# Head norms and memory softmax worked in place in PSUM, with small copies and scalings on ScalarE, in a two-layer hybrid decoder trunk

## The chip, the cores and the metric

The kernel runs on one core of one Trainium2 chip. It is timed as device microseconds of one execution, and the figure given is the median of several runs. Five engines matter: PE (TensorE: matmuls and transposes), DVE (VectorE), ACT (ScalarE), POOL (GpSimd) and SP, which issues the DMAs. SBUF is the working memory; PSUM holds the matmuls' results, in eight banks of 512 fp32 values for each of 128 partitions. Each engine runs its own instructions in a fixed order and waits on semaphores for the others.

## The reference

Two layers over 512 tokens of width 1024, all in fp32. Only what bears on the change is shown: rms norms of the heads with partial rotary embedding, the attention into 256 memory tokens, and the compressed branch of the sparse attention.

```python
def memory_attention(q, mem_n, w_kv, qnorm, knorm):
    k, v = jnp.split(mem_n @ w_kv, 2, axis=-1)
    q = rms_norm(q.reshape(Bz, S, M_HEADS, HEAD_DIM), qnorm)
    k = rms_norm(k.reshape(Bz, -1, M_HEADS, HEAD_DIM), knorm)
    s = jnp.einsum('bshd,bmhd->bhsm', q, k) * (HEAD_DIM ** -0.5)
    p = jax.nn.softmax(s, axis=-1)
    return jnp.einsum('bhsm,bmhd->bshd', p, v).reshape(Bz, S, M_WIDTH)
...
def even_layer(x, mem_n, pos, ...):
    q = rms_norm(b_q.reshape(Bz, S, B_HEADS, 2, B_QK_DIM), b_qnorm).transpose(0, 2, 3, 1, 4)
    k = rms_norm(b_k.reshape(Bz, S, B_HEADS, 2, B_QK_DIM), b_knorm).transpose(0, 2, 3, 1, 4)
    q, k = rope_partial(q, pos), rope_partial(k, pos)
...
def nsa(q, kv, gates, pos, ...):
    q = rope_partial(rms_norm(q, qnorm).transpose(0, 2, 1, 3), pos).reshape(Bz, G, R, S, hd)
    vc = compress(v_cmp_raw, cmp_idx, cmp_pos_v, cmp_w1_v, cmp_w2_v).transpose(0, 2, 1, 3)
...
def odd_layer(x, mem_n, pos, ...):
    gates = jax.nn.sigmoid(d_bg.reshape(Bz, S, D_HEADS, 3))
```

Layer 0 joins a chunked gating unit, a differential attention (8 heads of 32) and the memory attention (4 heads of 64). Layer 1 joins a convolution with 31 taps, a sparse attention (8 query heads of 64, compressed, selected and window branches) and again the memory attention. Each layer ends in one output projection.

## The kernel before

Tokens are taken in four tiles of 128. Every weight is fetched as fp32 and split into a high and a low half of the fast fp32r type: ACT copies the high half (L376), and the low half is the difference (L377), on POOL for the weights (tiles of 128x1024) and on DVE for activations. A product is then three matmuls (L396, L397, L398). PE does almost nothing else: transposes are matmuls too (L393).

The program is written as generators for the pieces of a layer (`mem_kv`, `b_qk`, `m_attn`, `d_kv`, `d_q`, `d_cmp`, `out_part` ...), which `merge` interleaves by rates and lead constants. The order in which each engine runs its instructions is then set at build by a list scheduler with priorities; nothing is reordered while it runs. A PSUM bank comes from a small pool of pages ("d", "t", "s", "c") and is given back once its last reader is done.

The pieces that the change touches:

- `head_norm` (L488): for 4 or 8 heads of 64. A projection's bank `p` is squared on ACT (L492), summed on DVE (L494), POOL makes the reciprocal root (`rstd`, L370 and L372), DVE multiplies `p` by gains or cosines into the SBUF tile `t` (L498 without rotary, L501 with), by sines into `u` (L503), and adds `u` crosswise to `t` (L504, L505). From there on the bank is free. It is called for the memory keys (`mem_kv`), the memory queries (`m_query`, used by `m_q` in layer 0 and `m_q1` in layer 1), the keys (`d_kv`) and queries (`d_q`) of layer 1: 12 passes without and 8 with rotary.
- `to_keys` (L511) and `to_queries` (L521) multiply `t` by the reciprocal root in SBUF; PE transposes the result, and L529/L530 copy it out as high and low halves (L530 on DVE).
- `b_qk` (L871 to L887) does the same for layer 0's heads of 32, in 16 passes: L873, L875, L878, L880, L881, L882, and at last L883, SBUF to SBUF.
- `m_attn` (L588): for each of two pairs of heads of a token tile, scores (L597/L598) into the bank `s`, the maximum (L600, DVE), exp (L603, ACT) into the SBUF tile `e`, the reciprocal of the sums (L604, DVE), and the scaling of `e` in place by `times`: the first head on DVE (L572), the second on POOL (L570). PE transposes `e`, and L582 to L584 multiply with the values. There are 16 such passes.
- `d_cmp` (L1111, L1115): compressed values copied to SBUF on ACT, and from there eight times 32x64 by DVE. `m_q1` (L1134): the gates' last step, DVE.

The convolution works around all this: for two of its four channel tiles, DVE adds 30 taps in PSUM (L1260); for one, ACT scales a tap (L1257) into one of two tiles `tmp`, and POOL adds it (L1258), so ACT's tap waits for POOL's add of two taps earlier.

## Time and profile before

| | |
|---|---|
| three runs, median (lowest to highest) | 735.17 us (733.96 to 738.78) |
| the profiled execution | 736.76 us, of which the span is 734.7 us |
| PE busy | 673.6 us, 92% of the span |
| DVE busy | 534.5 us, 73% |
| POOL busy | 388.5 us, 53% |
| ACT busy | 366.9 us, 50% |
| mean granted clock of TensorE | 0.979 of full speed |

Busy shares are averages over the whole span. A PE that counts as busy also counts the part of a matmul that overlaps the next one, so the idle time before single PE rows, given in brackets behind them with the instruction that ended it, tells more than the sum.

### The profile page before, as it was taken

What the parts mean: (1) busy time and instruction counts of PE and PEld (TensorE: products, weight loads), DVE (VectorE), ACT (ScalarE), POOL (GpSimd) and SP (SyncE); (2) the same over time, 40 slices, a digit from 0 to 9 for tenths busy, and PEclk for the clock granted to TensorE, in tenths of its full rate; (3) what the DMA queues carried; (4) which work ended last, traced back from release to release, by engine and by line L of the source; (5) the groups of instructions that cost most, each with busy time, mean ns of one, the idle gap of its engine ahead of it and who ended that gap; (6) DMA issues with size and microseconds to landing.
All of it is one profiled execution on the core that took longest, in us unless ns stands there. A gap on an engine that the chain in (4) does not pass through costs nothing.

```text
span 734.7 us, 10935 instructions
## 1 busy us (share of the span) xinstructions
PE 673.6 (92%) x3819; PEld 571.1 (78%) x3819; DVE 534.5 (73%) x1216; ACT 366.9 (50%) x819; POOL 388.5 (53%) x343
## 2 busy tenths in 40 slices
PE   4999999999999888999899899698697989989997
PEld 3789998788899767888787777586586878777885
DVE  4607787767867788952749939997959678888773
ACT  5344354555464664732534466432425566665651
POOL 3376985554366469524647389963625233511450
PEclk9999999999999999999999999999898999999999
DMA  8542254643231435222223111022211011110121
GB/s 307 162 143 73 69 148 111 186 115 119 72 116 59 143 115 200 76 71 58 92 86 118 56 58 58 29 90 83 83 34 58 29 58 31 63 52 1 58 72 72
DMA packets 22375, 66.55 MB, mean 91 GB/s; under 512 B 3504, under 2 KB 3760, under 8 KB 22320
## 3 DMA queue, kind: packets, MB, share of 16 engines
q1 hardware_dynamic: 22320, 65.86, 27.4%
q8 instruction: 30, 0.49, 0.3%
q14 instruction: 25, 0.20, 0.1%
HBM read 57.46 MB, written 2.10 MB: 81 GB/s over the span
## 4 chain that ended last, share of the span: by engine, by line
PE 59%; DVE 23%; POOL 7%; issue 4%; ACT 4%; DMA 2%; SPq 0%; POOLq 0%; DVEq 0%; ACTq 0%
PE banks L396 15%; PE banks L397 15%; PE banks L398 15%; PE banks L393 5%; DVE banks L1260 4%; PE banks L923 3%; DVE arena_r L377 2%; POOL arena_f L372 2%; POOL arena_r L377 2%; DMA arena_f<-in_wall_dram 2%; PE banks L1211 2%; ACT arena_r L376 2%; DVE arena_f L925 2%; PE banks L961 1%; POOL arena_f L1258 1%
## 5 line engine op out<-in xcount | busy, mean ns | idle before, releaser
L396 PE MATMUL banks<-arena_r 128*128 128x512 f32 (+2 forms) x784 | 293.5, 380 | 13.9 <-DVE arena_f L473 3.3
L397 PE MATMUL banks<-arena_r 128*128 128x512 f32 (+2 forms) x784 | 292.2, 374 | 4.2 <-POOL arena_r L377 3.1
L398 PE MATMUL banks<-arena_r 128*128 128x512 f32 (+2 forms) x784 | 290.7, 373 | 0.6 <-POOL arena_r L377 0.5
L377 POOL TENSOR_TENSOR arena_r<-arena_f,arena_r 128x1024 fp32r<-128x1024 f32 (+2 forms) x87 | 211.2, 2436 | 143.9 <-ACT arena_r L376 141.3
L396 PEld LDWEIGHTS banks<-arena_r 128*128 128x128 f32 x784 | 150.6, 193 | 40.3 <-ACT arena_r L376 5.2
L397 PEld LDWEIGHTS banks<-arena_r 128*128 128x128 f32 x784 | 150.4, 192 | 28.0 <-POOL arena_r L377 4.0
L398 PEld LDWEIGHTS banks<-arena_r 128*128 128x128 f32 x784 | 150.1, 192 | 24.7 <-POOL arena_r L377 1.4
L376 ACT ACTIVATE arena_r<-arena_f 128x1024 fp32r<-128x1024 f32 (+2 forms) x131 | 110.4, 854 | 80.8 <-PE banks L398 19.3
L393 PE MATMUL banks<-const,arena_f 128*128 128x128 f32 x507 | 83.5, 281 | 28.0 <-DVE arena_f L411 9.6
L393 PEld LDWEIGHTS banks<-const,arena_f 128*128 128x128 f32 x507 | 62.6, 146 | 39.0 <-DVE arena_f L411 10.1
L377 DVE TENSOR_TENSOR arena_r<-banks,arena_r 128x512 fp32r<-128x512 f32 (+1 forms) x112 | 67.0, 608 | 26.1 <-ACT arena_r L376 25.6
L376 ACT ACTIVATE arena_r<-banks 128x512 fp32r<-128x512 f32 (+1 forms) x112 | 57.8, 532 | 43.9 <-PE banks L393 27.1
L925 DVE CUSTOM_DVE_ANT_0 arena_f<-banks,const 128x512 f32<-128x512 f32 (+3 forms) x128 | 60.2, 484 | 21.1 <-PE banks L923 15.1
L372 POOL TENSOR_TENSOR arena_f<-arena_f,const 128x4 f32<-128x4 f32 (+3 forms) x60 | 68.6, 1146 | 3.6
L570 POOL TENSOR_SCALAR arena_f<-arena_f 128x256 f32<-128x256 f32 (+3 forms) x48 | 29.0, 609 | 74.2 <-DVE arena_f L1190 25.2
L1260 DVE SCALAR_TENSOR_TENSOR banks<-arena_f,const,banks 128x482 f32<-128x482 f32 (+14 forms) x90 | 66.0, 733 | 1.4
L954 ACT ACTIVATE arena_f<-arena_f 128x512 f32<-128x512 f32 (+3 forms) x64 | 35.8, 560 | 45.8 <-DVE arena_f L925 45.4
L923 PE MATMUL banks<-arena_r 128*128 128x512 f32 (+7 forms) x192 | 51.5, 345 | 4.2 <-DVE arena_f L925 4.1
L653 DVE TENSOR_TENSOR arena_f<-arena_f,banks 128x512 f32<-128x512 f32 x40 | 27.3, 684 | 29.0 <-PE banks L398 28.3
L1188 ACT ACTIVATE arena_f<-arena_f 128x512 f32<-128x512 f32 (+3 forms) x64 | 35.6, 558 | 24.2 <-DVE arena_f L925 24.2
L370 POOL TENSOR_SCALAR arena_f<-arena_f 128x4 f32<-128x4 f32 (+3 forms) x60 | 19.0, 317 | 47.9 <-DVE arena_f L494 15.8
L923 PEld LDWEIGHTS banks<-arena_r 128*128 128x128 f32 (+1 forms) x192 | 33.1, 193 | 9.0 <-DVE arena_f L925 5.9
(175 smaller groups left out, 847.0 us busy)
## 6 DMA issues: line engine op xcount, KB each, us to landing
arena_f<-in_wall_dram SPq DMA_DIRECT2D x88, 512.0 KB, 3.3
arena_r<-arena_r SPq DMA_DIRECT2D x96, 64.0 KB, 2.0
arena_f<-in_x_dram SPq DMA_DIRECT2D x7, 512.0 KB, 4.6
arena_f<-in_w_dram SPq DMA_DIRECT2D x4, 512.0 KB, 3.9
out_dram<-arena_f SPq DMA_DIRECT2D x8, 256.0 KB, 2.0
arena_f<-in_norms_dram SPq DMA_DIRECT2D x3, 512.0 KB, 4.7
arena_f<-in_mem_dram SPq DMA_DIRECT2D x2, 512.0 KB, 3.2
arena_f<-in_wqb_dram SPq DMA_DIRECT2D x2, 420.0 KB, 3.3
```

The lines of the kernel that those rows point to most:

```text
L372: G.tensor_tensor(r, v, mhalf[:parts, :n], ALU.pow)
L376: act(h, src, AF.Copy)
L377: (eng or V).tensor_tensor(l, src, f32(h), SUB)
L393: nc.tensor.transpose(o, i, ident[:k, :k])
L396: mm(o, lh, rh, start=first, stop=False)
L397: mm(o, lh, rl, start=False, stop=False)
L398: mm(o, ll, rh, start=False, stop=last)
L923: mm(t[:, a % per, :], q, k[:, :w], start=b == 0, stop=b == len(qk) - 1)
L925: V.tensor_tensor_reduce(e[a], t[:, a % per, :], cmask[:, S - w:], -1.0, -NEG, ADD, ALU.min, nm[:, a:a + 1])
L954: act(e[m], e[m], AF.Exp, bias=nm[:, m:m + 1], scale=-1.0, accum_out=l[:, i, m:m + 1])
L1188: act(es[j], es[j], AF.Exp, bias=nm[:, j:j + 1], scale=-1.0, accum_out=l[:, j:j + 1])
L1260: V.scalar_tensor_tensor(acc[:, z:], hc[:, :S - z], cw[:, f, k:k + 1], acc[:, z:], MUL, ADD)
```

## The change

All of `head_norm`'s and `b_qk`'s products and rotary adds are now written back into the projection's bank, and the last multiplication (`to_keys`, `to_queries`, L883) reads the bank and writes SBUF. The sine product is moved ahead of the in-place cosine product. In `m_attn` the exp is written in place into the score bank; the scaling reads the bank and writes `e`, on DVE for the first head and on ACT (a Copy with a per-partition scale) for the second; POOL has no part in it any more. The eight copies of `d_cmp` go from PSUM to their place on ACT, with the factor 0.5 in them, and so does the last step of the gates. The product with lambda in the differential attention (L957, L958) is as it was. Of the diff, what is left out are the callers, which only hand the three results of `head_norm` on.

```diff
@@ head_norm
         act(sq, p3, AF.Square)
+        if rope is not None:
+            cg, sg = rope
+            u = sc([P, nh, 16])
+            V.tensor_tensor(u, p3[:, :, 0:16], bc(sg.unsqueeze(1), [P, nh, 16]), MUL)
         ss = sc([P, nh])
         V.tensor_reduce(ss, sq, AX.X, ADD)
         r = rstd(sc, ss, 1.0 / 64, nh)
-        t = sq
         if rope is None:
-            V.tensor_tensor(t, p3, bc(gain.unsqueeze(1), [P, nh, 64]), MUL)
+            V.tensor_tensor(p3, p3, bc(gain.unsqueeze(1), [P, nh, 64]), MUL)
         else:
-            cg, sg = rope
-            V.tensor_tensor(t, p3, bc(cg.unsqueeze(1), [P, nh, 64]), MUL)
-            u = sc([P, nh, 16])
-            V.tensor_tensor(u, p3[:, :, 0:16], bc(sg.unsqueeze(1), [P, nh, 16]), MUL)
-            V.tensor_tensor(t[:, :, 0:8], t[:, :, 0:8], u[:, :, 8:16], ADD)
-            V.tensor_tensor(t[:, :, 8:16], t[:, :, 8:16], u[:, :, 0:8], ADD)
-        return t, r
+            V.tensor_tensor(p3, p3, bc(cg.unsqueeze(1), [P, nh, 64]), MUL)
+            V.tensor_tensor(p3[:, :, 0:8], p3[:, :, 0:8], u[:, :, 8:16], ADD)
+            V.tensor_tensor(p3[:, :, 8:16], p3[:, :, 8:16], u[:, :, 0:8], ADD)
+        return p3, r, sq
@@ to_queries
-        V.tensor_tensor(t, t, bc(r.unsqueeze(2), [P, nh, 64]), MUL)
+        V.tensor_tensor(t, q3, bc(r.unsqueeze(2), [P, nh, 64]), MUL)
@@ m_attn
-                        act(e[:, j, :], s[:, j, :], AF.Exp, bias=nm[:, j:j + 1], accum_out=l[:, j:j + 1])
+                        act(s[:, j, :], s[:, j, :], AF.Exp, bias=nm[:, j:j + 1], accum_out=l[:, j:j + 1])
                     V.reciprocal(l, l)
-                    for j in range(2):
-                        times(e[:, j, :], l[:, j:j + 1], SCALE_M[j])
+                    V.tensor_scalar(e[:, 0, :], s[:, 0, :], l[:, 0:1], None, MUL)
+                    act(e[:, 1, :], s[:, 1, :], AF.Copy, scale=l[:, 1:2])
@@ b_qk
-                V.tensor_tensor(t, p4, bc(bcg[:, i, :, :].unsqueeze(2), [P, 2, 4, 32]), MUL)
                 u = sc([P, 2, 4, 8])
                 V.tensor_tensor(u, p4[:, :, :, 0:8], bc(bsg[:, i, :, :].unsqueeze(2), [P, 2, 4, 8]), MUL)
-                V.tensor_tensor(t[:, :, :, 0:4], t[:, :, :, 0:4], u[:, :, :, 4:8], ADD)
-                V.tensor_tensor(t[:, :, :, 4:8], t[:, :, :, 4:8], u[:, :, :, 0:4], ADD)
-                V.tensor_tensor(t3, t3, bc(r.unsqueeze(2), [P, 8, 32]), MUL)
+                V.tensor_tensor(p4, p4, bc(bcg[:, i, :, :].unsqueeze(2), [P, 2, 4, 32]), MUL)
+                V.tensor_tensor(p4[:, :, :, 0:4], p4[:, :, :, 0:4], u[:, :, :, 4:8], ADD)
+                V.tensor_tensor(p4[:, :, :, 4:8], p4[:, :, :, 4:8], u[:, :, :, 0:4], ADD)
+                V.tensor_tensor(t3, p.rearrange("p (j d) -> p j d", d=32), bc(r.unsqueeze(2), [P, 8, 32]), MUL)
@@ d_cmp
-                vs = sc([64, 64])
-                act(vs, o, AF.Copy, scale=0.5)
                 G.memset(cbd, 0.0)
                 for g in range(2):
                     for r in range(4):
-                        V.tensor_copy(cbd[32 * r:32 * r + 32, g, r, :], vs[32 * g:32 * g + 32, :])
+                        act(cbd[32 * r:32 * r + 32, g, r, :], o[32 * g:32 * g + 32, :], AF.Copy, scale=0.5)
@@ m_q1
-                V.tensor_scalar(dgt[:, i, :, :].rearrange("p h b -> p (h b)"), th, 0.5, 0.5, MUL, ADD)
+                act(dgt[:, i, :, :].rearrange("p h b -> p (h b)"), th, AF.Copy, scale=0.5, bias=0.5)
```

Since the scheduler builds the order anew, rows move on every engine. Two places matter below. The names in the rows are the arenas: `banks` is PSUM, `arena_f` and `arena_r` are SBUF in fp32 and fp32r, `const` holds tables.

First DVE in `d_q`, the norm of the last token tile's queries, after which PE transposes them. Before:

```order
L377 TENSOR_TENSOR arena_r<-arena_f,arena_r 128x256 x2
L1260 SCALAR_TENSOR_TENSOR banks<-arena_f,const,banks 128x511
L377 TENSOR_TENSOR arena_r<-arena_f,arena_r 128x256 x2
L521 TENSOR_TENSOR arena_f<-arena_f 128x512
L494 TENSOR_REDUCE arena_f<-arena_f 128x8
L530 TENSOR_TENSOR arena_r<-banks,arena_r 64x2x128
L501 TENSOR_TENSOR arena_f<-banks,const 128x512
L503 TENSOR_TENSOR arena_f<-banks,const 128x128
L530 TENSOR_TENSOR arena_r<-banks,arena_r 64x2x128
L504 TENSOR_TENSOR arena_f<-arena_f 128x8x8
L505 TENSOR_TENSOR arena_f<-arena_f 128x8x8
L521 TENSOR_TENSOR arena_f<-arena_f 128x512
```

After (here L498 is the sum, L496 the sine product, L503 the cosine product, L504, L505 and L521 as before):

```order
L377 TENSOR_TENSOR arena_r<-arena_f,arena_r 128x256 x4
L496 TENSOR_TENSOR arena_f<-banks,const 128x128
L498 TENSOR_REDUCE arena_f<-arena_f 128x8
L530 TENSOR_TENSOR arena_r<-banks,arena_r 64x2x128
L503 TENSOR_TENSOR banks<-banks,const 128x512
L530 TENSOR_TENSOR arena_r<-banks,arena_r 64x2x128
L504 TENSOR_TENSOR banks<-banks,arena_f 128x8x8
L505 TENSOR_TENSOR banks<-banks,arena_f 128x8x8
L530 TENSOR_TENSOR arena_r<-banks,arena_r 64x2x128
L521 TENSOR_TENSOR arena_f<-banks,arena_f 128x512
```

The last tap (L1260) that stood here is gone from the stretch, since all taps now come earlier in DVE's order; the earlier tile's L521 has moved ahead of the four L377 rows, and three L530 copies instead of two stand between the sum and the last L521. Every product and add of the norm behind the sine product now has `banks` among its operands.

Then ACT at the start of the convolution's taps in layer 1, where the memory softmax is still running. Before (L603 is the exp, L1257 a tap's scaling):

```order
L603 ACTIVATE arena_f<-banks,arena_f 128x256 x4
L376 ACTIVATE arena_r<-arena_f 128x1024
L1257 ACTIVATE arena_f<-arena_f,const 128x482
L1257 ACTIVATE arena_f<-arena_f,const 128x483
L376 ACTIVATE arena_r<-banks 128x512
L603 ACTIVATE arena_f<-banks,arena_f 128x256 x2
L1257 ACTIVATE arena_f<-arena_f,const 128x484
L603 ACTIVATE arena_f<-banks,arena_f 128x256 x2
L1262 ACTIVATE arena_f<-banks 128x512
L1257 ACTIVATE arena_f<-arena_f,const 128x485
```

After (L601 is the exp, L604 the new scaling of the second head, L1252 a tap's scaling, L1230 another copy):

```order
L1252 ACTIVATE arena_f<-arena_f,const 128x486
L601 ACTIVATE banks,arena_f<-banks,arena_f 128x256
L376 ACTIVATE arena_r<-banks 128x512
L601 ACTIVATE banks,arena_f<-banks,arena_f 128x256 x3
L1252 ACTIVATE arena_f<-arena_f,const 128x487
L604 ACTIVATE arena_f<-banks,arena_f 128x256
L1252 ACTIVATE arena_f<-arena_f,const 128x488
L604 ACTIVATE arena_f<-banks,arena_f 128x256
L1252 ACTIVATE arena_f<-arena_f,const 128x489
L376 ACTIVATE arena_r<-arena_f 128x1024
L1252 ACTIVATE arena_f<-arena_f,const 128x490
L376 ACTIVATE arena_r<-banks 128x512
```

Before, the last exps stood beside the third tap. After, exps and scalings of the memory softmax stand between the fifth and the twelfth tap.

## Rows read from the trace of the kernel before

**Rows 1.** Page, part 1: busy us (share of span) and instructions, by engine:
```profile
PE 673.6 (92%) x3819; PEld 571.1 (78%) x3819; DVE 534.5 (73%) x1216; ACT 366.9 (50%) x819; POOL 388.5 (53%) x343
```

**Rows 2.** Page, part 4: shares of the chain that ended last, by engine:
```profile
PE 59%; DVE 23%; POOL 7%; issue 4%; ACT 4%; DMA 2%; SPq 0%; POOLq 0%; DVEq 0%; ACTq 0%
```

**Rows 3.** Timeline, PE then DVE, around 525: start us, us, instruction [idle before <-releaser]:
```profile
530.74 0.48 PE L393 MATMUL banks<-const,arena_f 128*128 128x128 f32 x1 [5.88 <-DVE arena_f L521]
...
525.39 0.22 DVE L504 TENSOR_TENSOR arena_f<-arena_f 128x64 f32<-128x64 f32 x1
525.53 2.39 DVE L505 TENSOR_TENSOR arena_f<-arena_f 128x64 f32<-128x64 f32 x1
528.02 2.66 DVE L521 TENSOR_TENSOR arena_f<-arena_f 128x512 f32<-128x512 f32 x1
```

**Rows 4.** Timeline, POOL, same stretch (xN: N in a row):
```profile
525.50 4.64 POOL L377 TENSOR_TENSOR arena_r<-arena_f,arena_r 128x1024 fp32r<-128x1024 f32 x2
```

**Rows 5.** Windows, all engines: busy us (x instructions), then granted clock PEclk, DMA:
```profile
530.70:534.60 3.90, 3.86 (x13) 3.32 (x14) 2.89 (x6) 1.77 (x5) 2.33 (x4) 0.50 0.44 134
```

**Rows 6.** By form, DVE, operands in SBUF: count | busy us, mean ns | idle before:
```profile
L572 DVE TENSOR_SCALAR arena_f<-arena_f 128x256 f32<-128x256 f32 x24 | 15.8, 670 | 0.3
L883 DVE TENSOR_TENSOR arena_f<-arena_f 128x256 f32<-128x256 f32 x16 | 14.0, 874 | 6.6 <-POOL arena_f L372 6.6
...
L511 DVE TENSOR_TENSOR arena_f<-arena_f 128x512 f32<-128x512 f32 x8 | 7.7, 965 | 0.7 <-POOL arena_f L372 0.5
...
L521 DVE TENSOR_TENSOR arena_f<-arena_f 128x256 f32<-128x256 f32 x8 | 6.7, 848 | 0.4 <-POOL arena_f L372 0.4
...
L521 DVE TENSOR_TENSOR arena_f<-arena_f 128x512 f32<-128x512 f32 x4 | 6.7, 1663 | 0.1
```

**Rows 7.** By source line, operand in PSUM: count, ns min/median/max, first and last start, forms:
```profile
L498 DVE TENSOR_TENSOR arena_f<-banks,const x12: 408/416/425, 227.0 to 389.8; 128x256 f32<-128x256 f32 x12
...
L473 DVE SCALAR_TENSOR_TENSOR arena_f<-arena_f,banks x20: 672/682/689, 124.5 to 653.2; 128x512 f32<-128x512 f32 x20
...
L1260 DVE SCALAR_TENSOR_TENSOR banks<-arena_f,const,banks x90: 706/733/755, 380.4 to 520.9; 128x482 f32<-128x482 f32 x3, 128x483 f32<-128x483 f32 x3, 128x484 f32<-128x484 f32 x3, 128x485 f32<-128x485 f32 x3
```

**Rows 8.** Timeline, DVE then PE, b_qk pass around 95:
```profile
95.39 2.59 DVE L883 TENSOR_TENSOR arena_f<-arena_f 128x256 f32<-128x256 f32 x1 [1.19 <-POOL arena_f L372]
...
98.13 0.41 PE L393 MATMUL banks<-const,arena_f 128*128 128x128 f32 x2 [1.05 <-DVE arena_f L883]
```

**Rows 9.** Timeline, DVE, two scalings of the memory softmax:
```profile
399.57 0.34 DVE L572 TENSOR_SCALAR arena_f<-arena_f 128x256 f32<-128x256 f32 x1
...
400.53 2.53 DVE L572 TENSOR_SCALAR arena_f<-arena_f 128x256 f32<-128x256 f32 x1
```

**Rows 10.** Timeline, PE, layer 1's memory attention:
```profile
417.96 0.39 PE L597 MATMUL banks<-arena_r 128*128 128x256 f32 x1 [0.53 <-ACT arena_f L603]
...
425.72 0.50 PE L396 MATMUL banks<-arena_r 128*128 128x512 f32 x1 [0.97 <-ACT arena_f L603]
```

**Rows 11.** Timeline, DVE, compressed values' copies in d_cmp:
```profile
551.24 3.82 DVE L1115 COPY const<-arena_f 32x64 f32<-32x64 f32 x8
```

**Rows 12.** Timeline, ACT then PE, around 470: a tap scaling, and PE:
```profile
469.35 0.72 ACT L1257 ACTIVATE arena_f<-arena_f,const 128x508 f32<-128x508 f32 x1 [1.48 <-POOL arena_f L1258]
...
470.61 0.27 PE L582 MATMUL banks<-arena_r 128*64 128x128 f32 x1 [2.49 <-ACT arena_r L376]
```

**Rows 13.** Timeline, PE then DVE, around 283: mem_kv(1):
```profile
283.52 0.50 PE L396 MATMUL banks<-arena_r 128*128 128x512 f32 x1 [2.42 <-DVE arena_f L498]
...
283.06 0.41 DVE L498 TENSOR_TENSOR arena_f<-banks,const 128x256 f32<-128x256 f32 x1
...
286.57 0.69 DVE L511 TENSOR_TENSOR arena_f<-arena_f 128x512 f32<-128x512 f32 x1
```

**Rows 14.** By source line, POOL's reciprocal root, and ACT's memory softmax exp:
```profile
L372 POOL TENSOR_TENSOR arena_f<-arena_f,const x60: 548/1010/2159, 5.5 to 567.6; 128x4 f32<-128x4 f32 x29, 128x8 f32<-128x8 f32 x20, 128x1 f32<-128x1 f32 x10, 64x1 f32<-64x1 f32 x1
...
L603 ACT ACTIVATE arena_f<-banks,arena_f x32: 463/474/492, 291.4 to 426.6; 128x256 f32<-128x256 f32 x32
```

More of the change, by code (lines that the diff above doesn't have):

```diff
@@ L495, in head_norm, with to_keys @@
         r = rstd(sc, ss, 1.0 / 64, nh)
-        t = sq
         if rope is None:
-            V.tensor_tensor(t, p3, bc(gain.unsqueeze(1), [P, nh, 64]), MUL)
+            V.tensor_tensor(p3, p3, bc(gain.unsqueeze(1), [P, nh, 64]), MUL)
         else:
-            cg, sg = rope
-            V.tensor_tensor(t, p3, bc(cg.unsqueeze(1), [P, nh, 64]), MUL)
-            u = sc([P, nh, 16])
-            V.tensor_tensor(u, p3[:, :, 0:16], bc(sg.unsqueeze(1), [P, nh, 16]), MUL)
-            V.tensor_tensor(t[:, :, 0:8], t[:, :, 0:8], u[:, :, 8:16], ADD)
-            V.tensor_tensor(t[:, :, 8:16], t[:, :, 8:16], u[:, :, 0:8], ADD)
-        return t, r
-    def to_keys(sc, t, r, h, l):
+            V.tensor_tensor(p3, p3, bc(cg.unsqueeze(1), [P, nh, 64]), MUL)
+            V.tensor_tensor(p3[:, :, 0:8], p3[:, :, 0:8], u[:, :, 8:16], ADD)
+            V.tensor_tensor(p3[:, :, 8:16], p3[:, :, 8:16], u[:, :, 0:8], ADD)
+        return p3, r, sq
+    def to_keys(sc, t, r, _, h, l):
         d = sc([P, 4, 2, 64])
@@ L516, in to_keys, with to_queries @@
         split(p, h, l)
-    def to_queries(sc, t, r, dst):
+    def to_queries(sc, q3, r, t, dst):
         nh = t.shape[1]
-        V.tensor_tensor(t, t, bc(r.unsqueeze(2), [P, nh, 64]), MUL)
+        V.tensor_tensor(t, q3, bc(r.unsqueeze(2), [P, nh, 64]), MUL)
         p = sc.ps("t", [P, nh // 2, P])
@@ L557, in mem_kv @@
             with SC() as sc:
-                t, r = head_norm(sc, p[:, 0:256], 4, mkg[layer], None)
-                to_keys(sc, t, r, kt[:, 0, :, tok(i)], kt[:, 1, :, tok(i)])
+                to_keys(sc, *head_norm(sc, p[:, 0:256], 4, mkg[layer], None), kt[:, 0, :, tok(i)], kt[:, 1, :, tok(i)])
             yield UT
@@ L564, in m_query @@
         with SC() as sc:
-            t, r = head_norm(sc, p, 4, mqg[layer], None)
-            to_queries(sc, t, r, [qs[:, :, tok(i)]])
+            to_queries(sc, *head_norm(sc, p, 4, mqg[layer], None), [qs[:, :, tok(i)]])
     def times(e, f, eng):
@@ L1039, in d_kv @@
             with SC() as sc:
-                t, r = head_norm(sc, p[:, 0:256], 4, None, (dcg[:, i, 1, :], dsg[:, i, 1, :]))
-                to_keys(sc, t, r, dkh[:, :, tok(i)], dkl[:, :, tok(i)])
+                to_keys(sc, *head_norm(sc, p[:, 0:256], 4, None, (dcg[:, i, 1, :], dsg[:, i, 1, :])), dkh[:, :, tok(i)], dkl[:, :, tok(i)])
             yield UT + 440
@@ L1046, in d_q @@
             with SC() as sc:
-                t, r = head_norm(sc, p, 8, None, (dcg[:, i, 0, :], dsg[:, i, 0, :]))
+                n = head_norm(sc, p, 8, None, (dcg[:, i, 0, :], dsg[:, i, 0, :]))
                 qsc = SC()
@@ L1050, in d_q @@
                 dqs[i] = (q, qsc)
-                to_queries(sc, t, r, [q[:, 0:4, :], q[:, 4:8, :]])
+                to_queries(sc, *n, [q[:, 0:4, :], q[:, 4:8, :]])
             yield UT + 880
@@ L1365 @@
 PTILE, WIDE = 1, 2
-SCALE_D, SCALE_M = "vp", "vp"
+SCALE_D = "vp"
 CD, CX = 80, 3600
```

## The prediction

> **What bounds the kernel now.** I read the page's busy shares first, then the chain, then the idle times in front of single PE rows in the timeline, then what the releasing engine did meanwhile. PE is busy for 92% of the span [rows 1], so at most some 61 us of idle are to be had, and the chain that ended last runs through PE for 59% and through DVE for 23% [rows 2]: where PE does wait, DVE is mostly what it waits for. The clearest such place is the norm of the last query tile in layer 1. PE's transposes at 530.74 begin after 5.88 us of idle that L521 ended [rows 3]. Its chain on DVE took 0.22 us for L504, but 2.39 for its twin L505 and 2.66 for L521 [rows 3], while POOL ran two weight splits of 4.64 us together from 525.50 on [rows 4]. L505 began at 525.53 and L521 at 528.02, and both ended with one of the splits. The reader is to see an instruction that reads two SBUF tensors and is held for the rest of a split. Right behind this wait TensorE ran at a granted clock of 0.50, that is 1.2 GHz instead of 2.4, with 13 matmuls in 3.9 us [rows 5].
>
> **Who is held, and who is not.** The forms on changed lines whose operands are all in SBUF have means far over an undisturbed one: L883 874 ns, L511 965, L521 848 and 1663, the scalings L572 670 [rows 6]. DVE instructions that take an operand from PSUM never show it: L498 lies between 408 and 425 ns over 12 instructions, L473 between 672 and 689 over 20, L1260, which also writes PSUM, between 706 and 755 over 90 [rows 7]. I take the PSUM rows as the undisturbed price: 0.42 us for 256 columns, 0.68 for 512. Then the time lost to splits is 14.0 - 16 x 0.42 = 7.3 us on L883, 7.7 - 8 x 0.68 = 2.3 on L511, 6.7 - 8 x 0.42 = 3.3 and 6.7 - 4 x 0.68 = 4.0 on L521, and, with 0.35 undisturbed [rows 9], 15.8 - 24 x 0.35 = 7.4 on L572, of which two thirds (16 of 24, the others belong to the differential attention) are 4.9 [rows 6]. With 2.1 for the one L505 and 2.3 for d_cmp's copies (3.82 instead of 8 x 0.19, my value for the six undisturbed ones) [rows 3, 11] that is about 26 us of DVE's 534.5. The change puts a PSUM operand into every one of them or moves it to ACT. At DVE's share of the chain, 26 x 0.23 = 6 us: a first size. L377 between SBUF tensors, the lambda product and the differential attention's scalings stay as they were, and stay exposed.
>
> **The sum, part by part, against the profiled run's 736.76 us.**
> - d_q, last tile: L505 2.39 to 0.28 (0.22 and the write into PSUM), L521 2.66 to 0.68: -4.1. PE still waits some 1.8. Bounds: -2, if the third L530 that now stands ahead and the queue take half back, and -5.88, all of it.
> - The half clock behind it: 3.9 us at half speed cost up to 1.95 [rows 5]. A wait of 1.8 may still bring it, but after a much shorter pause; between 0 and -1.95 I take -1.5.
> - b_qk: L883 at 95.39 took 2.59 and PE waited 1.05 for it [rows 8]. Undisturbed it ends 2.2 earlier: -1.05, the whole wait.
> - Memory softmax of layer 1: the scaling at 400.53 took 2.53, its neighbour 0.34 [rows 9]. PE waits of 0.53 and 0.97 for the exps [rows 10] come from DVE running late. But the score bank is now held until both scalings have read it, longer by a reciprocal and a scaling of 0.42 to 0.47 [rows 7, 14]. Bounds -3 and +1.5; -1.0.
> - The scaling out of PSUM costs DVE more: 0.42 at 256 columns instead of 0.34 [rows 7, 9], 16 times 0.08 = 1.3 us, at DVE's 23% +0.3. The Trainium skill has this rule too, on its page "VectorE: DVE Perf Modes", section "Mode 2×_2P": an instruction with one tensor input can use both read ports only from SBUF, since PSUM has one. By its doubled rate the undisturbed scaling should gain about half of its per-element time in SBUF; the row shows a fifth of the whole, fixed cost included, and the sum goes by the row.
> - In-place writes: L1260 against L473 is 0.05 each [rows 7]. Three a pass, 24 passes with rotary: 3.6 us of DVE, most of it under PE's work: +0.3, bounds 0 and +0.8.
> - d_cmp: 3.82 us leave DVE [rows 11]; eight copies on ACT, at most 0.47 each by the longer exp row [rows 14], on an engine busy for 50% [rows 1]. Bounds 0 and -1; -0.5. The four gates' steps with them, 0.
> - The other DVE time saved, about 26 - 12 named here = 14 us: at 23% 3, but b_qk warns that 7.3 us of lost time on L883 gave one visible wait of 1.05; 0 to -3, I take -2.0, since the products of L511 and L521 go straight into transposes.
> - Banks held longer: before, L498 freed the bank at 283.47, and PE went on at 283.52 after 2.42 us of idle [rows 13]. The bank is now free when L511 ends, 287.26 in the old times: +3.8 if nothing else moved. L498 itself will come earlier, and elsewhere the new order has more PE work in between: +1.0, bounds 0 and +3.8.
> - Memory softmax among the taps on ACT: the tap at 469.35 came 1.48 us late since it waited for POOL [rows 12]. Five exp or scaling groups now stand behind such taps; one of them showing is +1.5, bounds 0 and +7.4.
>
> POOL loses 16 scalings, which nobody waited for as far as the rows show: 0. The sum is -4.1 - 1.5 - 1.05 - 1.0 + 0.3 + 0.3 - 0.5 - 2.0 + 1.0 + 1.5 = -7.05, hence 729.7. The profiled run lies 1.6 over the median of 735.17, so for a median 728.1.
>
> **The rivals.**
> *The gain was covered (no change).* If the 5.88 us is not given back, because the next SBUF instruction in DVE's order (an L377, say) takes the same split's rest, or PE meets the next late producer, only b_qk's 1.05 and 1 or 2 us more are left, and the two additions of 2.5 us eat them: 733 to 736. For it speaks that 7.3 us lost on L883 gave about 1 of PE idle; against it, that in d_q three instructions in a row ahead of the transposes have no such neighbour.
>
> *The banks are held too long (slower).* From the last product on, a bank waited for nothing; now it also waits for POOL's root, 1.0 us at the median of L372 and up to 2.2 [rows 14], which queues behind splits, and then for the last multiplication. There are 36 passes (12, 8 and 16). At mem_kv(1) alone this is 3.8 us. If PE has as little slack at one pass in six, 6 x 3.8 = 23 us are added, and the forecast without its own +1.0 becomes 728 + 22 = 750. It decides from about three such passes on (11 us against the gain of 7). For it: the 2.42 us wait on exactly this bank. Against it: only that bank shows a PE wait for L498, and the order was built anew with the longer hold in it.
>
> *The softmax is caught among the taps (slower).* If all five groups behind a tap show in PE, 5 x 1.48 = 7.4 us instead of 1.5, and each wait of over 2 us may be followed by a half clock like that of [rows 5], 1.95 each. Three of those make 728.1 + 5.9 + 5.9 = 740, and five 744; PE's wait of 2.49 for an ACT row at 470.61, ACT itself being behind taps, shows that it happens [rows 12]. Against it: PE has other work in the merge. The Trainium skill's page "ScalarE: Activation LUTs", section "Rules for kernel authors", says to use VectorE and not ScalarE for a plain multiplication; its figure for a pointer operand gives an estimate of 0.49 us at 256 columns, and by it alone all 16 scalings would cost 16 x 0.07 = 1.1 us more than on DVE. The exp's row of 0.47, also with a pointer operand, agrees with the figure [rows 14].
>
> **The numbers.** The forecast, 722 to 733 about 728.1, has 0.46; better than it, 714 to 722, if the DVE time saved pays at more than its share and the clock with it, 0.16; covered, 733 to 736, 0.20; banks, 743 to 751, 0.09; taps, 739 to 744, 0.09. A measurement of this kernel tells about 1%, 7.35 us, from no change: faster is below 727.8, slower above 742.5. Half of the forecast, 0.23, and the better case are faster, 0.39; its other half, the covered case and nearly half of the tap case are the same, 0.47; the rest is slower, 0.14. For 8 in 10 the range leaves out half of the better case, the banks and the worst of the taps: 718 to 742; the forecast's own is 722 to 733.
>
> **What would show it.** L505 and L521 of d_q's last tile below 0.8 us each and PE's wait there under 2.5; no row on a changed line over 0.8 us; DVE's busy time down by some 22 us (26 less the writes and the slower scalings), and ACT's up by 16 x 0.47 = 7.5 us and the small copies. Wrong would be: PE waits released by L511, L521 or L883 in front of a projection's matmul (L396): banks; or by an exp or scaling behind L1252: taps; or the gain at 530 lost again within 20 us.

## The result and the profile after

The changed kernel takes 717.3 us (715.1 to 718.3, 4 runs) against 736.0 for the one before: a ratio of 0.9724, 95% interval 0.9696 to 0.9753. It is faster by some 19 us, where 7 had been forecast.

The page of the changed kernel, busy times and then the chain's shares by engine:

```profile
PE 673.4 (94%) x3819; PEld 572.6 (80%) x3819; DVE 511.8 (72%) x1204; ACT 375.7 (53%) x846; POOL 375.0 (52%) x327
...
PE 74%; DVE 8%; ACT 5%; POOL 5%; DMA 4%; issue 2%; SPq 1%; ACTq 0%; POOLq 0%
```

DVE is busy for 22.7 us less than in [rows 1], which is the amount forecast, ACT for 8.8 more. PE's busy time is as it was (673.4 against 673.6); what the span lost is idle time of PE. In the chain DVE fell from 23% [rows 2] to 8.

The changed lines by source (count, shortest, median and longest in ns), with L881 the final multiplication of b_qk and L603 the scaling of the first head:

```profile
L505 DVE TENSOR_TENSOR banks<-banks,arena_f x8: 191/207/232, 458.2 to 516.4; 128x32 f32<-128x32 f32 x4, 128x64 f32<-128x64 f32 x4
...
L521 DVE TENSOR_TENSOR arena_f<-banks,arena_f x12: 415/425/692, 235.3 to 517.0; 128x256 f32<-128x256 f32 x8, 128x512 f32<-128x512 f32 x4
...
L881 DVE TENSOR_TENSOR arena_f<-banks,arena_f x16: 403/423/425, 74.0 to 134.7; 128x256 f32<-128x256 f32 x16
...
L511 DVE TENSOR_TENSOR arena_f<-banks,arena_f x8: 676/684/692, 273.6 to 486.8; 128x512 f32<-128x512 f32 x8
...
L603 DVE TENSOR_SCALAR arena_f<-banks,arena_f x16: 471/484/485, 291.4 to 435.8; 128x256 f32<-128x256 f32 x16
```

None of these rows is held: the longest is 0.69 us, where before single ones took 2.4 to 2.7 [rows 3, 8, 9]. The end of d_q's last norm, PE, then DVE, then POOL's splits next to it:

```profile
517.80 1.28 PE L393 MATMUL banks<-const,arena_f 128*128 128x128 f32 x8
...
516.44 0.23 DVE L505 TENSOR_TENSOR banks<-banks,arena_f 128x64 f32<-128x64 f32 x1
517.04 0.69 DVE L521 TENSOR_TENSOR arena_f<-banks,arena_f 128x512 f32<-128x512 f32 x1
...
510.14 2.41 POOL L377 TENSOR_TENSOR arena_r<-arena_f,arena_r 128x1024 fp32r<-128x1024 f32 x1
...
517.58 2.39 POOL L377 TENSOR_TENSOR arena_r<-arena_f,arena_r 128x1024 fp32r<-128x1024 f32 x1 [0.95 <-ACT arena_r L376]
```

In [rows 3] PE waited 5.88 us there; now the transposes begin with no idle time to show, 0.1 us after L521. These rows alone do not show that the operands did it: in the new order no split ran while L504 and L505 did, and the next one began only near the end of L521. The scaling from PSUM costs 0.48, not the 0.42 that I took from a plain product.

Layer 0 is slower. PE meets two waits that the kernel before did not have, one for a DMA that stacks parts of the queries or keys, and one for DVE's pass over a block of scores (L923, mask and row maximum), which frees a score bank:

```profile
93.33 0.47 PE L921 MATMUL banks<-arena_r 96*128 96x512 f32 x1 [1.99 <-DMA arena_r<-arena_r]
...
132.87 0.44 PE L921 MATMUL banks<-arena_r 96*128 96x384 f32 x1 [1.13 <-DVE arena_f L923]
```

The gain in the middle shows in windows of PE and DVE (busy us of each engine, then the granted clock), first before, then after. By 437 us PE has begun 2396 instructions in both kernels, and by 455 us 2495 and 2496, so the third window holds the same place of the program; the first two are a few us apart:

```profile
395.00:410.00 15.00, 13.49 (x70) 10.95 (x69) 14.72 (x24) 7.70 (x21) 6.06 (x6) 1.00 0.20 71
410.00:425.00 15.00, 12.80 (x78) 9.95 (x76) 14.89 (x22) 4.89 (x13) 7.53 (x6) 1.00 0.21 70
455.00:475.00 20.00, 13.62 (x76) 10.92 (x75) 19.17 (x38) 11.03 (x20) 19.06 (x17) 0.96 0.08 26
```

```profile
395.00:410.00 15.00, 15.00 (x73) 12.61 (x73) 14.12 (x27) 8.44 (x20) 9.30 (x7) 1.00 0.44 140
410.00:425.00 15.00, 15.00 (x100) 12.96 (x98) 14.57 (x24) 9.81 (x22) 9.54 (x6) 1.00 0.22 71
455.00:475.00 20.00, 18.68 (x112) 15.36 (x111) 19.52 (x42) 10.66 (x19) 17.77 (x18) 1.00 0.09 27
```

The reader is to see DVE: it was busy for 98%, 99% and 96% of these windows, and PE for 90%, 85% and 68%. PE now has no idle time in the first two windows and 7% in the third; DVE is still busy for 94%, 97% and 98%.

### The profile page after: what moved, and what is told of

Its sections match the earlier page's. It is cut to its first block, busy times and chain, and to the rows that moved or that the text cites. A ratio compares the mean times of both kernels' runs of the same rounds, so it can differ in the third digit from the quotient of the medians.

```text
span 715.1 us, 10919 instructions
## 1 busy us (share of the span) xinstructions
PE 673.4 (94%) x3819; PEld 572.6 (80%) x3819; DVE 511.8 (72%) x1204; ACT 375.7 (53%) x846; POOL 375.0 (52%) x327
## 4 chain that ended last, share of the span: by engine, by line
PE 74%; DVE 8%; ACT 5%; POOL 5%; DMA 4%; issue 2%; SPq 1%; ACTq 0%; POOLq 0%
PE banks L397 19%; PE banks L396 19%; PE banks L398 19%; PE banks L393 6%; POOL arena_r L377 3%; PE banks L921 3%; DMA arena_f<-in_wall_dram 3%; PE banks L1206 2%; ACT arena_r L376 2%; PE banks L959 2%; DVE arena_r L377 1%; PE banks L1176 1%; DVE banks L1255 1%; POOL arena_f L372 1%; DVE arena_f L923 1%
## 5 line engine op out<-in xcount | busy, mean ns | idle before, releaser
L377 POOL TENSOR_TENSOR arena_r<-arena_f,arena_r 128x1024 fp32r<-128x1024 f32 (+2 forms) x87 | 210.7, 2431 | 183.5 <-ACT arena_r L376 178.1
L377 DVE TENSOR_TENSOR arena_r<-banks,arena_r 128x512 fp32r<-128x512 f32 (+1 forms) x112 | 67.2, 609 | 17.4 <-ACT arena_r L376 17.0
L923 DVE CUSTOM_DVE_ANT_0 arena_f<-banks,const 128x128 f32<-128x128 f32 (+3 forms) x128 | 60.2, 485 | 26.6 <-PE banks L921 20.7
L921 PE MATMUL banks<-arena_r 128*128 128x256 f32 (+7 forms) x192 | 50.4, 339 | 9.5 <-DVE arena_f L923 7.3
L952 ACT ACTIVATE arena_f<-arena_f 128x512 f32<-128x512 f32 (+3 forms) x64 | 35.6, 558 | 38.7 <-DVE arena_f L923 37.9
L1183 ACT ACTIVATE arena_f<-arena_f 128x256 f32<-128x256 f32 (+3 forms) x64 | 35.7, 559 | 28.7 <-DVE arena_f L923 28.3
L568 POOL TENSOR_SCALAR arena_f<-arena_f 128x512 f32<-128x512 f32 (+3 forms) x32 | 19.5, 616 | 49.4 <-DVE arena_f L1185 37.6
L370 POOL TENSOR_SCALAR arena_f<-arena_f 128x4 f32<-128x4 f32 (+3 forms) x60 | 16.0, 266 | 50.3 <-ACT arena_f L406 16.8
```

Source lines behind the costliest of these rows:

```text
L377: (eng or V).tensor_tensor(l, src, f32(h), SUB)
L921: mm(t[:, a % per, :], q, k[:, :w], start=b == 0, stop=b == len(qk) - 1)
L923: V.tensor_tensor_reduce(e[a], t[:, a % per, :], cmask[:, S - w:], -1.0, -NEG, ADD, ALU.min, nm[:, a:a + 1])
L952: act(e[m], e[m], AF.Exp, bias=nm[:, m:m + 1], scale=-1.0, accum_out=l[:, i, m:m + 1])
L1183: act(es[j], es[j], AF.Exp, bias=nm[:, j:j + 1], scale=-1.0, accum_out=l[:, j:j + 1])
```

## The experiments

Ten of the seventeen hold the order fixed. Their program is traced twice: once as it stands, to learn the order that the scheduler gives each engine, and once with the edit, with every engine's instructions chained to that order by ordering edges. In this way an operand's place can be changed and nothing else, save that in norms worked in place the sine product trades places with the cosine product. Passes for which a longer held bank would make such an order deadlock stay as they are.

**One part alone, in an order of the scheduler's own.** Each is the kernel before with one part of the diff shown ahead.

```diff
@@ only_softmax: before, with the m_attn part
@@ only_headnorm: before, with the head_norm, to_keys and to_queries part
@@ only_bqk: before, with the b_qk part
@@ only_copies: before, with the d_cmp and m_q1 parts
```

> The kernel before with the memory softmax part alone (exp in place in PSUM, first head scaled by DVE out of PSUM, second by ACT). Theory 1, held DVE instructions: DVE saves about 5 us of held time in the scalings (16 of them) and PE gets back what hung on them in layer 1's memory attention; 732 to 735. Theory 2, DVE is the bound of the stretch 395 to 475 us, where the trace of before has it busy for 14.7 and 14.9 of 15 us and then 19.2 of 20: all time taken off DVE there counts, and POOL's freed time lets the taps run earlier; 724 to 728. Theory 3, the new order does it: anything within 727 to 742, and the single parts will not add up.

> The kernel before with the 20 head norms in place in PSUM alone. Theory 1: the wait of 5.9 us for L521 in d_q's last tile and the half clock behind it go, mem_kv loses 1 to 4 by the longer bank hold; 729 to 732. Theory 2: the head norms of d_kv and d_q lie partly in the DVE-bound stretch (455 to 475), so a few us more; 725 to 729. Theory 3: 727 to 742, without a pattern.

> The kernel before with layer 0's query and key norms in place in PSUM alone. Theory 1: 7.3 us of held time on L883 go, but only one wait of 1.05 us hung on them: 734 to 736. The bank theory: the new kernel is behind the old by some 4 to 5 us between 80 and 230 us, and this part with its longer held banks is what does it; 739 to 741. Theory 3: 730 to 742.

> The kernel before with the eight compressed-value copies and the gates' last step on ACT alone. Theory 1: 3.8 us leave DVE at 551 to 555; behind them before had PE waits of 1.0 and 2.7 us and a half clock of 6.8 us at 560 to 569, which a DVE chain some 3 us earlier takes away: 729 to 732. My prediction's small term (-0.5): 735 to 736. Theory 3: 730 to 742.

Measured, as ratios to before: softmax 0.9937 (0.9905 to 0.9968), head norms 0.9823 (0.9751 to 0.9894), b_qk 1.0075 (1.0042 to 1.0109), copies 0.9872 (0.9814 to 0.9930). The four sum to -22 us, close to the whole -20 (0.9724). b_qk, which had the most held time of all (7.3 us), makes the kernel slower; the copies, my term of -0.5, give 9. The sum alone does not say whether operands or orders did it.

**Operands against order.** Before's order with PSUM operands, and after's order with SBUF operands:

```diff
@@ order_inplace (order of before; 10 of 16 b_qk passes, 15 of 20 head norms, 16 scalings, 8 copies)
+        NEW = inplace("h")
...
-        t = sq
+        t = p3 if NEW else sq
...
-                        V.tensor_copy(cbd[32 * r:32 * r + 32, g, r, :], vs[32 * g:32 * g + 32, :])
+                            V.tensor_scalar(cbd[32 * r:32 * r + 32, g, r, :], o[32 * g:32 * g + 32, :], 0.5, None, MUL)
@@ afterorder_sbuf (order and engines of after; 16 b_qk passes, 19 of 20 head norms, 16 first heads)
-            V.tensor_tensor(p3, p3, bc(cg.unsqueeze(1), [P, nh, 64]), MUL)
+            V.tensor_tensor(t, p3, bc(cg.unsqueeze(1), [P, nh, 64]), MUL)
```

> The order of before on every engine, instruction for instruction, but with PSUM operands wherever that order allows it without a deadlock: 10 of the 16 passes of b_qk, 15 of the 20 head norms (the last query tile among them), the first head's scaling in all 16 memory softmax passes, and the eight copies of d_cmp read PSUM on DVE. No instruction changes its engine or its place, except that the sine product trades places with the cosine product. Held theory: DVE's time falls by some 18 of the 26 us, the wait for L521 at 530 shrinks from 5.9 to about 2, and the time is 727 to 731. Order theory: the gain of the change came with the new order, and this stays at 734 to 737. DVE-bound theory: as held, but with the 455 to 475 us stretch also better; 723 to 727.

> The converse: the order and the engines of the changed kernel, instruction for instruction, but DVE's operands back in SBUF (all 16 passes of b_qk, 19 of 20 head norms, exp and scaling of the first head in all 16 softmax passes). Banks are free as early as before. Held theory: POOL's splits hold DVE again, DVE's busy time is back by some 15 to 22 us, and the time is 726 to 732. Order theory: 716 to 720. Bank theory: the loss of some 4 us in layer 0 disappears here, since the banks are not held; together with the order theory 712 to 716.

Measured: 0.9864 (0.9823 to 0.9905), that is 726.8 us, and 0.9937 (0.9898 to 0.9977), 732.3. DVE's busy time in the first, and in the second:

```profile
PE 670.8 (92%) x3819; PEld 568.7 (78%) x3819; DVE 517.3 (71%) x1216; ACT 370.0 (51%) x819; POOL 385.9 (53%) x343
```

```profile
PE 677.4 (93%) x3819; PEld 572.5 (78%) x3819; DVE 536.2 (74%) x1204; ACT 374.3 (51%) x846; POOL 378.7 (52%) x327
```

The first is 17 us under before, the second 24 over after: the held time goes and comes back with the operands, in either order. In the order of before a part of the gain is given back at the banks. The rows of PE in order_inplace (L903 is its L883, L524 its L511, L534 its L521):

```profile
130.79 0.50 PE L405 MATMUL banks<-arena_r 128*128 128x512 f32 x1 [2.05 <-DVE arena_f L903]
...
270.97 0.50 PE L405 MATMUL banks<-arena_r 128*128 128x512 f32 x1 [2.64 <-DVE arena_f L524]
...
395.69 0.58 PE L610 MATMUL banks<-arena_r 128*128 128x256 f32 x1 [2.39 <-DVE arena_f L534]
...
524.77 0.66 PE L402 MATMUL banks<-const,arena_f 128*128 128x128 f32 x4 [1.17 <-DVE arena_f L534]
```

Three waits of 2.05, 2.64 and 2.39 us now stand in front of projections and scores, released by the last multiplication that reads a bank. That is the bank rival, of the kind it named. The fourth row is d_q's: 1.17 us are left of 5.88. Here two splits do run beside L518 (the former L505) and L534, and with an operand in PSUM neither is held:

```profile
523.69 0.23 DVE L518 TENSOR_TENSOR banks<-banks,arena_f 128x64 f32<-128x64 f32 x1
524.03 0.69 DVE L534 TENSOR_TENSOR arena_f<-banks,arena_f 128x512 f32<-128x512 f32 x1
...
523.39 4.68 POOL L386 TENSOR_TENSOR arena_r<-arena_f,arena_r 128x1024 fp32r<-128x1024 f32 x2
```

In afterorder_sbuf, the order of after with SBUF operands, the same two instructions (L516 and L532 there) take 0.22 and 0.69 us as well, since no split runs beside them, and PE waits 0.64 us:

```profile
527.74 0.22 DVE L516 TENSOR_TENSOR arena_f<-arena_f 128x64 f32<-128x64 f32 x1
...
528.46 0.69 DVE L532 TENSOR_TENSOR arena_f<-arena_f 128x512 f32<-128x512 f32 x1
```

So at this place either change is enough: the operands in the old order, or the new order.

**Each term alone, in the order of before.**

```diff
@@ order_dq: in place only in d_q (8 heads)
@@ order_copies: only the copies read PSUM, on DVE
@@ order_softmax: only the first head's exp and scaling
@@ order_norms4: only head norms of 4 heads (those that the order allows)
@@ order_bqk10: only 10 of the 16 passes of b_qk
@@ all but order_dq choose their passes by a list
+    return NEW and n in PASSES.get(kind, ())
```

> The order of before on every engine; only the four norms of d_q are in place in PSUM. My sum's first two terms alone (-4.1 for L505 and L521, -1.5 for the half clock behind): 731 to 733. If the gain is taken back within 30 us by the next late producer: 735 to 737. If the chain that hangs on it is longer than I thought: 726 to 730.

> The order of before on every engine; only the eight compressed-value copies read PSUM (still on DVE, with the factor 0.5). Alone and with a new order, the copies and the gates on ACT gave 9 us. Held theory: two held copies cost 2.3 us, and the PE waits of 1.0 and 2.7 us and the half clock behind them hang on that: 730 to 734. My prediction's -0.5: 735 to 737. Order theory: 735 to 738, since the 9 us came from the new order.

> The order of before on every engine; only the first head's exp and scaling of the 16 memory softmax passes are in place in PSUM (the second head stays on POOL). My term: -1.0, with the score bank held longer as its counterweight: 735 to 737 against 736.9. If the held scalings (4.9 us of DVE) pay in full because DVE is the bound there: 730 to 733. If the longer held bank outweighs it: 738 to 741.

> The order of before on every engine; only those head norms of four heads that this order allows (memory keys and queries, and layer 1's keys) are in place. My terms: +1.0 for the banks and a part of the -2.0 for the rest: 735 to 738. Bank theory, the waits for L511 and L521 in front of projections that the run with all of it showed at 271 and 396 us: 738 to 742. Held theory with little bank cost: 732 to 735.

> The order of before on every engine; only 10 of the 16 passes of b_qk are in place. My term: -1.05, the wait for L883 at 95: 735 to 737. Bank theory, a wait of 2.3 us for L883 before a projection as the run with all of it showed at 131 us: 737 to 740. With the scheduler's new order the whole edit cost 5.5 us; if it were the banks, this would be over 740.

Measured: d_q 0.9952 (0.9927 to 0.9976), copies 0.9934 (0.9908 to 0.9959), softmax 0.9994 (0.9962 to 1.0026), four-head norms 1.0015 (0.9976 to 1.0055), b_qk 1.0024 (0.9991 to 1.0057). Two of five terms are told from nothing. DVE's busy time fell by 2.0, 2.5, 3.5, 4.0 and 3.8 us in these traces: 4.5 us less on DVE gave 8.4 us of time in the first two, and 11.3 less gave nothing that shows in the other three. In the copies' run DVE does all eight in half the time of [rows 11], and PE has one wait left where before it had two:

```profile
549.34 1.82 DVE L1136 TENSOR_SCALAR const<-banks 32x64 f32<-32x64 f32 x8
```

```profile
560.00 0.66 PE L402 MATMUL banks<-const,arena_f 128*128 128x128 f32 x2 [1.80 <-DVE arena_f L1183]
```

The same place before, and the clock behind the second wait:

```profile
560.63 0.66 PE L393 MATMUL banks<-const,arena_f 128*128 128x128 f32 x4 [1.04 <-DVE arena_r L530]
...
563.96 0.66 PE L393 MATMUL banks<-const,arena_f 128*128 128x128 f32 x2 [2.68 <-DVE arena_f L1160]
```

```profile
562.00:568.80 6.80, 4.84 (x12) 3.62 (x13) 5.98 (x18) 3.09 (x8) 2.98 (x4) 0.50 0.20 78
```

The copies stand on DVE ahead of a chain of small softmax steps for which PE waits twice, and TensorE then ran at 0.50, 1.2 GHz, for 6.8 us. The second wait hangs on a row that the change does not touch: L1157, a step of 128x8, is held for 2.31 us before, and in the copies' run the step two rows on (L1182) is:

```profile
560.61 2.31 DVE L1157 TENSOR_SCALAR arena_f<-arena_f 128x8 f32<-128x8 f32 x1
```

```profile
557.15 2.24 DVE L1182 TENSOR_TENSOR arena_f<-arena_f,const 128x8 f32<-128x8 f32 x1
```

So the shorter copies move the chain ahead, and take away the first wait and a part of the second; behind it the clock is 0.76 over 7 us (558 to 565), so some 3.4 us of half clock are left of 6.8.

**Why b_qk costs.**

```diff
@@ bqkorder_sbuf (against before; NEW gives the order of only_bqk, and is off in what runs)
+                d4 = p4 if NEW else t
...
+                V.tensor_tensor(d4, p4, bc(bcg[:, i, :, :].unsqueeze(2), [P, 2, 4, 32]), MUL)
@@ undo_bqk: after, with b_qk as before
```

> The kernel with b_qk alone in place (742.5 against 737.2 of before) with the same order on every engine, but its products in SBUF again, so that banks are free early and L883 can be held by splits. Bank theory (the loss comes from banks held until L883): back to 735 to 738. Order theory (the loss comes from the order that the scheduler built around the edit): stays at 741 to 745, or worse by what held instructions cost.

> The changed kernel with b_qk as before, everything else in place or on ACT. If the parts add up as they did alone (softmax -5, head norms -13, copies -9, b_qk +5.5 us), 712 to 714, faster than the changed kernel. If b_qk's loss belongs to an order that this scheduler run does not give again, 715 to 721.

Measured: 1.0089 (1.0061 to 1.0117) and 0.9724 (0.9682 to 0.9767). With operands and banks as before, the order alone costs 6.6 us, about as much as b_qk in place in that order (1.0075). So the order is enough for the loss; longer held banks and shorter instructions together change nothing that shows. The trace shows the waits of the changed kernel's layer 0 again:

```profile
93.60 0.47 PE L925 MATMUL banks<-arena_r 96*128 96x512 f32 x1 [1.15 <-DMA arena_r<-arena_r]
...
133.00 0.45 PE L925 MATMUL banks<-arena_r 96*128 96x384 f32 x1 [1.14 <-DVE arena_f L927]
```

Undoing b_qk in the changed kernel does not make it faster; its ratio is that of the changed kernel. In its trace the loss in layer 0 is gone (PE's 1338th instruction begins at 232.8 us, against 240.1 in the changed kernel and 235.1 before), but by the 1911th most of that is lost again (346.6, 347.8 and 343.0). The parts do not simply add where the scheduler is free.

**Is it held time?** A cut of each weight split in two leaves every operand where it was:

```diff
@@ split, on POOL (order_split2; the line below stays for DVE)
+            n = l.shape[1] // 2
+            eng.tensor_tensor(l[:, :n], src[:, :n], f32(h[:, :n]), SUB)
+            x = eng.tensor_tensor(l[:, n:], src[:, n:], f32(h[:, n:]), SUB)
...
         (eng or V).tensor_tensor(l, src, f32(h), SUB)
@@ order_split2: before with this, order of before; order_both: with the operands of order_inplace too
@@ after_split2, after_split4: after with this in two, in four, in an order of the scheduler's own
```

> The kernel before, in its own order on every engine and with all operands in SBUF, but each weight split on POOL cut into two instructions of half the width, one right behind the other (87 become 174). Held theory: a DVE instruction that reads two SBUF tensors is held until POOL's present instruction ends, so the longest L521, L505 and L883 fall from 2.4 to 2.7 us to about 1.4 to 1.9, DVE's busy time falls by 30 to 45 us (the unchanged lines gain too) and the time by 6 to 12 us: 725 to 731. If DVE is not held by POOL but slowed by something else of that length, nothing changes but POOL's fixed cost: 736 to 741.

> The order of before on every engine, with both edits at once: PSUM operands as in order_inplace (726.8 against 737.0) and weight splits cut in two as in order_split2 (716.4 against 736.9). Held theory: the two take the same time away, so the second one gives less than alone; in-place operands on top of cut splits give 0 to 5 us, 711 to 717, and the longer held banks may eat it: up to 719. If in place pays for another reason than held instructions, the gains add: 704 to 708.

> The changed kernel with each weight split on POOL cut in two. What is still held in it (L377 between SBUF tensors, the lambda product and others, some 53 us in DVE's sum over the fastest) should halve. Held theory, with DVE on 8% of the changed kernel's chain: 2 to 6 us faster, 711 to 716. Order theory: the scheduler sees other durations and builds another order, 712 to 726. If POOL's extra fixed cost (87 more instructions) reaches PE through the weights: 718 to 724.

> The changed kernel with each weight split on POOL cut in four. Cutting in two gave 711.0. Held theory: what is held halves again, 708 to 711. POOL's fixed cost, 260 more instructions of some 0.1 us, reaches PE through late weights: 711 to 716.

Measured: order_split2 0.9729 (0.9702 to 0.9756), 716.4 us; order_both 0.9714 (0.9688 to 0.9740), 716.7; after_split2 0.9652 (0.9634 to 0.9669), 711.0; after_split4 0.9736 (0.9684 to 0.9788), 714.9. Busy times of order_split2, and by source its L883 (L889 here) and L521 (L527):

```profile
PE 672.7 (94%) x3819; PEld 571.5 (80%) x3819; DVE 506.4 (71%) x1216; ACT 367.3 (51%) x819; POOL 406.1 (57%) x430
```

```profile
L889 DVE TENSOR_TENSOR arena_f<-arena_f x16: 408/426/1505, 73.9 to 130.1; 128x256 f32<-128x256 f32 x16
...
L527 DVE TENSOR_TENSOR arena_f<-arena_f x12: 412/553/1586, 225.6 to 512.0; 128x256 f32<-128x256 f32 x8, 128x512 f32<-128x512 f32 x4
```

The longest L883 took 2.59 us [rows 8] and now takes 1.51; the longest L521 2.66 [rows 3] and now 1.59. DVE is busy for 28 us less, POOL for 18 more, and the time falls by 20. So the holds are POOL's splits: half as long a split, and the longest hold is shorter by as much. A part of the 20 may come from the first half of a weight being ready earlier. That was not separated, but PE's waits that end with a split on POOL fell only from 3.6 to 1.1 us in all. Four cuts are worse than two in the changed kernel: POOL is busy for 43 us more than without a cut (418.2 against 375.0 us), 0.17 us for each of 261 more instructions; whether that is the reason was not shown. The cut in two, after_split2, is the fastest version found.

In place on top of the cut gives nothing in all. That does not mean that the two edits take the same time away, as the places show. The table has the time (us) at which PE begins its nth instruction, one trace each. The order of PE is the same in the first four rows, and the same in the last two; between these two groups places are compared by count.

| | 2293rd | 2675th | 2866th | 3057th | last |
|---|---|---|---|---|---|
| before | 416.1 | 494.6 | 544.9 | 586.7 | 730.5 |
| order_inplace | 418.1 | 493.2 | 538.7 | 577.9 | 721.5 |
| order_split2 | 401.3 | 478.3 | 528.8 | 571.0 | 711.5 |
| order_both | 410.5 | 486.4 | 530.8 | 571.0 | 711.6 |
| afterorder_sbuf | 428.7 | 499.7 | 545.5 | 581.8 | 725.2 |
| after | 420.9 | 487.1 | 532.5 | 568.8 | 710.9 |

The cut gains 16.3 us by the 2675th instruction and nothing from there to the 3057th. In place at the same order is 2 us behind at the 2293rd, and gains some 7.5 from the 2675th to the 3057th, a stretch that holds d_q and d_cmp. With both, in place takes 9.2 of the cut's 14.8 us back by the 2293rd, where PE's waits for held banks stand again (2.06, 2.38 and 1.52 us), and gives some 7.5 between the 2675th and the 3057th. That the totals agree is a balance of the two.

## Why the prediction was wrong

The direction held, and so did the mechanism of the hold; the size did not: 717.3 lies under the range (718 to 742), and -7 was -19. What the prediction gave as its signs came true: L505 and L521 under 0.8 us, no changed row over 0.8, DVE down by 22.7 us, ACT up by 8.8. The result lies in its better case (714 to 722, 0.16), whose condition was that DVE's time pays at more than its share.

At the order of before, the sum without the taps' +1.5 is -8.55, and order_inplace, with what that order allows, measured -10.0 (-7.0 to -13.0). So the total was fair there, but not term by term, and that it fits is luck. What fell short were two terms of the sum: the memory softmax among the taps, and d_cmp.

- **The memory softmax among the taps** was the step that failed most. The sum took the new order as a cost there (+1.5, with -1.0 and +0.3 for the softmax itself, so +0.8; the -2.0 for what no row named may lie here in part) and put what it gains at nothing. From PE's 2293rd to its 2675th instruction, 416 to 495 us before, the 78.5 us became 66.2: -12.3. The taps did not catch the softmax: PE is busy for 15.00 of 15 us in the windows at 395 and 410. With in-place operands at the order of before the same stretch takes 75.1 us, with SBUF operands at the order of after 71.0: 3.4 us come from the operands, 7.5 from the order and the moves to ACT. The window from 455 to 475, where I saw only a risk, shows it: PE's 13.62 us of 20 became 18.68. With in-place operands at the order of before, and with SBUF operands at the order of after (2507 PE instructions are begun at 467 there), it is

```profile
455.00:475.00 20.00, 15.16 (x81) 12.11 (x80) 19.51 (x41) 10.49 (x20) 19.02 (x18) 0.91 0.08 26
```

```profile
467.00:487.00 20.00, 17.35 (x100) 13.80 (x99) 19.77 (x38) 9.95 (x18) 17.05 (x16) 1.00 0.07 26
```

- **d_cmp**: -0.5, measured -4.9 at a fixed order (-3.0 to -6.8) and -9 with the scheduler free. I had counted DVE's 3.8 us and not followed what stands behind them: two PE waits of 1.04 and 2.68 us, the second behind a held row that the change does not touch, and a half clock of 6.8. In the changed kernel the stretch with it, from the 2866th to the 3057th instruction, is 5.5 us shorter.
- **The worth of held time**: I found 26 us of it, and the 22.7 us that DVE lost agree. DVE's 23% of the chain gave a first size of 6 us, and the part not named by rows entered at 2 of 14. Measured: 22.7 us less on DVE went with 18.7 in the changed kernel, 17.2 with 10 in order_inplace, 28 with 20 in order_split2. But no single rate holds: two terms paid nearly double, three paid nothing. That DVE was busy for 96 to 99% in the windows above does not explain it either: the scalings of the softmax were held there (two of them for 2.53 and 1.82 us), and order_softmax took 3.5 us off DVE for nothing that shows. One size was misread: the 16 scalings of the memory softmax take 12.23 us together (290 to 440 us), so 6.6 were lost and not 4.9; the other eight lie at 663 to 687 us, in layer 1. And L521 in [rows 3] did not end with the split, but 0.5 us behind it.
- **d_q**: forecast -5.6 with its half clock, measured -3.5 alone at a fixed order (-1.8 to -5.4). The mechanism and the place were right, the size a little high; 1.17 us of wait were left where I said 1.8, and the clock behind it stayed at 1.00. From the 2675th to the 2866th instruction the changed kernel gains 4.9 us, but so does the order of after with SBUF operands (4.5).
- **b_qk**: -1.05, measured +1.8 alone with an interval that holds 0, and +5.5 with its own order, for a reason that none of my rivals had: the order built around the edit. The changed kernel is 4.8 us behind at its 2293rd instruction.
- **Softmax** (-1.0 and +0.3) and **four-head norms** with their banks (-2.0 and +1.0): at a fixed order both are within the noise; those sizes were fair.
- **Banks held**: +1.0, and the rival at 23 us. At the order of before the rival shows in three waits of 7.1 us together. In the changed order PE waits for L511 for 1.6 us in all (two rows). That the scheduler knew of the longer hold and put PE work in between, which I had named as what speaks against the rival, fits, but was not shown.

How PSUM operands and order share the 19 us depends on what is taken first: operands in the old order give 10, of which the copies 5; the new order with SBUF operands gives 5, and it has the copies on ACT too. By the table the new order with SBUF operands is 12.6 us behind before at the 2293rd instruction and makes up 17.9 behind it. The PSUM operands, put into that order, give 7.8 us back ahead of the 2293rd instruction, 4.8 up to the 2675th and 1.7 behind. Which of the scheduler's choices loses time in the first part and gains it in the second was not taken apart; that cause stays open.

## What to carry to other kernels

Where instructions of one engine are stretched by another's long ones, no share prices them: not their engine's share of the chain, and not its busy share in the stretch. Follow the engine's order from each held row to the PE wait that hangs on it, and to the clock behind that wait; held rows that the edit does not touch stand in that chain too. Two places paid nearly double here, and three nothing. Cutting the long instruction in two was worth as much as moving the operands of the short ones, though at other places, and cost a few lines. An edit to a kernel with a scheduled order is two edits; tracing it twice and chaining the old order separates them. The new order can be a gain, so a sum that enters it only as a risk is one-sided.

## What the runs showed of the hardware

DVE's products, scalings and copies with all their tensors in SBUF were held for the rest of a POOL split that ran: at most 2.59 us for L883 behind splits of 2.4, and 1.51 behind splits of 1.3 to 1.4. Those with an operand in PSUM were not: L881 took 0.40 to 0.43 us over 16, and L518 and L534 of order_inplace 0.23 and 0.69 beside two splits. Row sums that read SBUF alone (L494) were not held either: 0.41 to 0.69 us over 20 in the kernel before, five of which began during a split. The Trainium skill, page "SBUF — State Buffer", section "Who interferes with whom", says that a DVE instruction with two SBUF inputs contends with a GpSimd instruction that reads SBUF, and that whichever starts second waits for the whole of the other. The rows of L883, L505 and L521 agree for a DVE instruction that starts second. The scaling of [rows 9], with one tensor input in SBUF, was held as well (2.53 us), which the same section puts down to DVE's mode with two ports. Not expected was the price of cutting: two halves of 128x512 take 2.69 us together (113.8 + 111.8 us for 84) where one of 128x1024 took 2.44.
